# Two FFNs: sums of up-projection weight blocks made in HBM ahead of their tiles, and five more tiles by seven block products

## The chip, the core and the metric

One core of a Trainium2 chip runs the whole program. The metric is device time in microseconds (us) of one execution. All inputs lie in HBM when it starts; all arithmetic is in float32, which TensorE handles as float32r: each operand is split into a high and a low part, and a product takes three matmuls (high·high, high·low, low·high).

## The reference, cut to what matters

A two-layer decoder trunk on 512 tokens and 1024 features. Each layer has a mixer, then a gated FFN, then a gated per-layer embedding. The change is in the FFN, and in the weights that it loads:

```python
def conv_ffn(xn, w_up, conv_w, conv_b, w_down):        # xn: 512 x 1024
    h = xn @ w_up                                       # 1024 x 5632, gate half and linear half
    hp = jnp.pad(h, ((0, 0), (CONV_WIDTH - 1, 0), (0, 0)))
    c = conv_b + sum(hp[:, t:t + S] * conv_w[t] for t in range(CONV_WIDTH))
    g, u = jnp.split(c, 2, axis=-1)
    return (jax.nn.silu(g) * u) @ w_down                # 2816 x 1024
```

## The kernel before, in words

**Tiles.** The 2816 hidden features of an FFN are 22 tiles `j` of 128. For a tile, the kernel needs 256 columns of `w_up` (128 gate, 128 linear), which is 1 MB: 128 partitions by 8 blocks of input features by 2 blocks of 128 columns. The tiles go in three parts, 0-7, 8-15 and 16-21 (`PARTS`); after each part comes the product with the rows of `w_down` that belong to it. One tile of each next part (8 and 16) is computed ahead of that product.

**A plain tile** (`up`, `mm3`) takes 8 x 2 x 3 = 48 matmuls of 128x512, named `up` in the profile. **A woven tile** (`woven_up`) groups features and tokens in 2 x 2 blocks and takes seven block products instead of eight (Winograd's form of Strassen's scheme): 7 x 4 x 3 = 84 matmuls of 128x256, named `ux` and `uy`. For that it needs four combinations of the weight blocks, made by three adds of VectorE (`weave`, L163 to L165) into a buffer `wsum`. Its weights are split in four units, three of 1024 columns and one of 512, where a plain tile has two of 1024. Its results go to SBUF by five copies of ScalarE and two adds of VectorE (L812, L813; tiles `head` and `tail`, in the profile `gate`/`line` or `out..h`/`out..l`). Before, the tiles in `UPS` are woven in both layers: 7, 8, 9, 10, 12, 14, 16, 17, 18, 20, 21.

**Weights.** SyncE's queue brings pieces of 1 MB from HBM into three staging buffers (`staged`, `load`; `wraw`, and `wsum` takes one of the three too). Unit by unit, ScalarE casts the high part (`wh`, L203) and VectorE subtracts it for the low part (`wl`, L204) into a ring of four buffers each (`pump`, `WBUFS`), so that the split runs four units ahead of TensorE. A load starts once its staging buffer is free, that is when the last `wl` that reads it is done.

**Order.** Each engine runs its instructions in the order in which it is given them; `behind` pins an instruction behind another on one engine. GpSimd does little: norm sums (`nf0acc`, `np0acc`, `n1acc`), an inverse root for each norm (`nf0rt`, `n1rt`), and the DMAs on its own queue. Those on L600 add to what is at the destination (`accum_op=ALU.add`): `saved<-head`, `saved<-tail`, `h<-head`, `h<-tail`, of 256 KB each. The root `n1rt`, in the stage of the first layer's gate and the K projection, goes by VectorE's `n1hl` and `n1d` to a matmul `n1sp`, which spreads it over the partitions.

Of the kernel before, what the change touches and what calls it, by code (L numbers as in the profile page):

```python
# [52 lines left out]
def tile_yoco(ctx: ExitStack, tc: tile.TileContext, t, out: bass.AP, out_b: bass.AP):  # L53
    nc = tc.nc
# [13 lines left out]
        return mmp.tile([P, S], F32, tag="mm", name=name)  # L68


    pieces, paired, woven, beside = [], set(), set(), set()

    def plan(ap_, n, cols, own=None):
# [23 lines left out]
    def plan_woven(w, n_chunks, k0, k1):  # L97

        for c in range(n_chunks):
            n = (k1 - k0) * P  # L100
            woven.add(len(pieces))
            pieces.append((w[c, :, k0 * 256 : k1 * 256], 2 * n, [(0, n)] * 3 + [(0, n // 2)], None))

    def plan_ups(l, j0, j1):
        for j in range(j0, j1):
            (plan_woven if j in UPS else plan_cols)(t["w_up"][l, j : j + 1], 1, *((0, KD) if j in UPS else (KD,)))

    def plan_ffn(l):
        plan(t["pT"][l], 2 * S, S, own=[(mp, "m4", "m5")])
# [31 lines left out]
    state = {"raw": 0, "unit": 0, "next": 0, "tags": [0, 1, 2], "turn": 2, "pt": 0, "sent": {}}  # L141

    def behind(ins, front):

        tc.add_manual_dep(ins.ins, front.ins.name,
                          mybir.DependencyInfo(mybir.DependencyClass.NoSync, mybir.DependencyReason.DATA),
                          reason="order")

    def staged(name):
        tags = state["tags"]  # L150
        r = wp.tile([P, 2 * UNIT], F32, tag=f"r{tags[state['turn'] % len(tags)]}", bufs=1, name=name)
        state["turn"] += 1
        return r

    def weave(i, q):


        n = pieces[i][1] // 4
        g = raws[i][:, : 4 * n].rearrange("p (k b m) -> p b k m", b=4, m=P)
        if q == 0:  # L160
            s = sums[i] = staged(f"wsum{i}")[:, : 4 * n].rearrange("p (b k m) -> p b k m", b=4, m=P)
            k = n // P
            nc.vector.tensor_add(s[:, 0::3], g[:, 1:2].to_broadcast([P, 2, k, P]), g[:, 0::3])  # L163
            nc.vector.tensor_add(s[:, 2], s[:, 3], g[:, 0])
            nc.vector.tensor_add(s[:, 1], s[:, 2], g[:, 2])  # L165
        return (g[:, 0:3:2], sums[i][:, 2:4], sums[i][:, 0:2], g[:, 3:4])[q]

    def load(upto, queue=nc.sync):
        while state["raw"] < min(upto, len(pieces)):
            j = state["raw"]  # L170
            a, m = pieces[j][:2]
            r = raws[j - 1][:, UNIT:] if j in beside else staged(f"wraw{j}")
            ins = queue.dma_start(r[:, :m].rearrange("p (c m) -> p c m", c=2) if j in paired else r[:, :m], a)
            for front in state["sent"].pop(j, []):
                behind(ins, front)
            raws[j] = r
            state["raw"] += 1
# [145 lines left out]
    class Norm:  # L323
# [11 lines left out]
        def square(self, k, eng=None):  # L335
            sq = tp.tile([P, S], F32, tag="sq", name=f"{self.name}sq{k}")
            box["squared", k] = ins = nc.scalar.activation(sq, h[k], AF.Square)
            if self.acc is None:
                self.acc = sq
            else:  # L340
                acc = tp.tile([P, S], F32, tag="acc", name=f"{self.name}acc{k}")
                self.added = (eng or nc.gpsimd).tensor_add(acc, self.acc, sq)
                self.acc = acc
            return ins

# [99 lines left out]
        def rstd(self):  # L445

            r = tp.tile([P, S], F32, tag="rstd", name=f"{self.name}rstd")
            if self.line is not None:
                nc.gpsimd.dma_start(r, self.line.partition_broadcast(P))
            else:  # L450
                nc.scalar.copy(r, self.spread(0, S // 64))
            return r

    def inv_root(ms, name, scale=1.0, n=None):
        if n is None:
            n = ms.shape[1]
            ms = [(slice(None), ms)]
        m = const.tile([P, n], F32, tag=f"ms{n}", bufs=2, name=f"{name}m")
        for some, x in ms:
            box["m"] = nc.vector.tensor_scalar(m[some, :], x, scale, EPS, op0=ALU.mult, op1=ALU.add)  # L460
        r = const.tile([P, n], F32, tag=f"rt{n}", bufs=2, name=f"{name}rt")
        nc.gpsimd.tensor_tensor(r, m, minus_half[:, :n], op=ALU.pow)
        return r

    box = {}
# [264 lines left out]
    def ffn(l, norm, nxt):  # L730
# [56 lines left out]
        def woven_up(j, later):  # L787

            product = products(ins)
            n = PAIRS * P  # L790
            chain, other = psum(f"ux{j}")[:, first], psum(f"uy{j}")
            if j in ASIDE:
                head, tail = couple(ASIDE[j], f"out{j}", F32)
# [11 lines left out]
            nc.scalar.copy(side, other[:, second])  # L805
# [6 lines left out]
            nc.vector.tensor_sub(tail[:, second], tail[:, second], side)  # L812
            nc.vector.tensor_add(head, head, other)  # L813
            return (head, tail) if later else gated(j, (head, tail))
# [91 lines left out]
    def ple(l, norm, nxt, pe):  # L906
        xs = norm.xs[0][0]
        rstd, held = None, []
        for c in range(4):
            parts = chunk(256, KD)  # L910
# [114 lines left out]
    edge = at.tile([P, PAIRS, 2, N], F32R, tag="vtl", name="edge")  # L1025
    us = [Pair(c, edge, f"us{c}", range(3 * PAIRS)) for c in range(PAIRS)]
    for c in range(4):
        parts = chunk(256, KD)
        ups = [psum(f"u{c}_{j}") for j in range(2)]
        for j in range(2):  # L1030
# [47 lines left out]
    for k in range(KD):  # L1078
        nm.split(k, 1)
        if k == 3:  # L1080
            nm.turn()
    rt = nm.begin(rows=2)

    state["tags"] = [0, 1]
    parts = chunk(256, KD)
# [1 line left out]
    mm3(qps[0], parts, xq, 0)  # L1087
    rstd = nm.rstd()
    mm3(qps[1], parts, xq, P)

    for j in range(2):
        kf = tp.tile([P, S], F32, tag="acc", name=f"kf{j}")
# [314 lines left out]
    r = [f"r{(state['turn'] + j) % 3}" for j in range(3)]  # L1407
# [229 lines left out]
```

## Time and profile before

| | |
|---|---|
| median of 3 runs (lowest to highest) | 1100.43 us (1099.83 to 1101.02) |
| the profiled execution's own time | 1100.39 us |
| its span in the profile | 1098.7 us |
| granted TensorE clock | 0.999 |
| TensorE busy | 1089.1 us (99%) |
| VectorE busy | 959.0 us (87%) |
| ScalarE busy | 661.0 us (60%) |
| GpSimd busy | 125.0 us (11%) |
| moved by DMA | 144.24 MB, mean 131 GB/s |

A row of a group of instructions gives line, engine, operation, tiles and shapes, the count, then total busy us and mean ns of one. A row of a timeline gives start and length in us. In a row of waits stand the total, the times and the longest. A row by windows gives, after the stretch and its length, the busy time and count of PE, PEld, VectorE (DVE), ScalarE (ACT) and GpSimd (POOL), those that have instructions there, then granted clock, DMA share and GB/s. A row of DMA issues gives the count, KB of each and median us from issue to landing.

### The profile page before, as it was taken

The page shows a single profiled execution, that of the slowest core. Times are in us where ns is not written, and L with a number is a line of the kernel's source. Part 1 is how long each engine was busy: PE and PEld are TensorE (multiplying, and loading weights), DVE is VectorE, ACT ScalarE, POOL GpSimd, SP SyncE. Part 2 cuts the span into 40 slices and gives each one's busy share as a digit, 9 for nine tenths or more (in the row PEclk, how much of TensorE's full clock was granted, in tenths as well). Part 3 has the DMA queues.
Part 4 walks back from the last instruction along what each step waited for, and adds up shares of the span by engine and source line. Part 5 has one row for each costly group of instructions (what it writes and reads, how often), then busy time and mean ns, then how long its engine had stood idle before and what let it go on. Part 6 is the DMA issues. An engine that isn't in the chain of part 4 may idle for free.

```text
span 1098.7 us, 17476 instructions
## 1 busy us (share of the span) xinstructions
PE 1089.1 (99%) x6629; PEld 974.4 (89%) x6629; DVE 959.0 (87%) x1540; ACT 661.0 (60%) x1141; POOL 125.0 (11%) x192
## 2 busy tenths in 40 slices
PE   9999999999999999999999999999999999999997
PEld 7888988899998999988888887888999989999886
DVE  5588889999899989877988997799998999898887
ACT  5735666565676656655656775565655666567544
POOL 2200200000100010021114452000001000100200
PEclk9999999999999999999999999999999999999999
DMA  9621674125633267353234216441255333664534
GB/s 317 113 88 39 178 264 150 43 77 116 155 115 116 79 160 222 120 190 112 67 87 135 78 58 227 176 153 39 77 142 128 115 116 86 156 220 142 203 95 98
DMA packets 47508, 144.24 MB, mean 131 GB/s; under 512 B 13048, under 2 KB 18688, under 8 KB 36928
## 3 DMA queue, kind: packets, MB, share of 16 engines
q1 hardware_dynamic: 40560, 128.77, 35.6%
q0 software_dynamic: 5296, 9.70, 6.7%
q10 hardware_dynamic: 1568, 4.65, 1.1%
q8 instruction: 52, 0.85, 0.3%
q14 instruction: 32, 0.26, 0.1%
HBM read 116.89 MB, written 18.88 MB: 124 GB/s over the span
## 4 chain that ended last, share of the span: by engine, by line
PE 95%; DVE 2%; issue 1%; ACT 1%; DMA 0%; SPq 0%; POOLq 0%; POOL 0%; ACTq 0%
PE up L234 20%; PE ux L234 10%; PE dx L234 10%; PE uy L234 8%; PE dy L234 8%; PE d L234 6%; PE q L234 4%; PE gate L234 4%; PE u L234 4%; PE o L234 4%; PE up L750 2%; PE pv L1326 1%; PE v L244 1%; PE v L245 1%; PE v L246 1%; PE pin L234 1%
## 5 line engine op out<-in xcount | busy, mean ns | idle before, releaser
L204 DVE TENSOR_TENSOR wl<-wraw,wh 128x1024 fp32r<-128x1024 f32 (+2 forms) x198 | 217.3, 1102 | 42.8 <-ACT wh L203 41.9
L203 ACT CAST wh<-wraw 128x1024 fp32r<-128x1024 f32 (+2 forms) x197 | 182.8, 933 | 107.6 <-PE up L234 21.8
L203 ACT CAST wh<-wsum 128x1024 fp32r<-128x1024 f32 x84 | 88.3, 1052 | 62.7 <-issue 14.9
L204 DVE TENSOR_TENSOR wl<-wsum,wh 128x1024 fp32r<-128x1024 f32 x84 | 102.5, 1225 | 16.1 <-ACT wh L203 16.0
L762 DVE SCALAR_TENSOR_TENSOR c<-up,vec,c 128x511 f32<-128x511 f32 (+1 forms) x88 | 65.0, 744 | 2.4 <-ACT c L760 1.9
L234 PE MATMUL up<-nf10h,wh 128*128 128x512 f32 x160 | 62.3, 389 | 0.0
L234 PE MATMUL up<-nf00h,wh 128*128 128x512 f32 x160 | 62.3, 389 | 0.0
L234 PE MATMUL up<-nf10l,wh 128*128 128x512 f32 x160 | 62.3, 389 | 0.0
L234 PE MATMUL up<-nf00l,wh 128*128 128x512 f32 x160 | 62.3, 389 | 0.0
L234 PE MATMUL up<-nf00h,wl 128*128 128x512 f32 x160 | 62.1, 389 | 0.0
L234 PE MATMUL up<-nf10h,wl 128*128 128x512 f32 x160 | 62.0, 389 | 0.0
L600 POOL DMA_DIRECT2D saved<-head x16 | 13.9, 871 | 412.9 <-DVE head L720 412.9
L760 ACT ACTIVATE c<-up,vec 128x512 f32<-128x512 f32 x44 | 34.0, 777 | 31.8 <-PE up L234 26.6
L163 DVE TENSOR_TENSOR wsum<-wraw 128x1024 f32<-128x1024 f32 x42 | 51.2, 1220 | 0.6
L234 PE MATMUL ux<-t,wh 128*128 128x256 f32 x264 | 50.4, 283 | 0.0
L234 PEld LDWEIGHTS ux<-t,wh 128*128 128x128 f32 x264 | 41.2, 192 | 0.0
L234 PE MATMUL ux<-t,wl 128*128 128x256 f32 x132 | 37.4, 283 | 0.0
L234 PEld LDWEIGHTS up<-nf00h,wl 128*128 128x128 f32 x160 | 30.0, 188 | 6.2
L234 PEld LDWEIGHTS up<-nf10h,wl 128*128 128x128 f32 x160 | 30.0, 188 | 6.2
L234 PEld LDWEIGHTS up<-nf00l,wh 128*128 128x128 f32 x160 | 30.0, 188 | 6.2
L234 PEld LDWEIGHTS up<-nf10l,wh 128*128 128x128 f32 x160 | 30.0, 188 | 6.2
L234 PEld LDWEIGHTS up<-nf10h,wh 128*128 128x128 f32 x160 | 30.0, 188 | 6.0
(769 smaller groups left out, 3734.3 us busy)
## 6 DMA issues: line engine op xcount, KB each, us to landing
wraw<-in_w_up SPq DMA_DIRECT2D x44, 1024.0 KB, 5.6
wraw<-in_w_down SPq DMA_DIRECT2D x16, 1024.0 KB, 5.0
wraw<-in_w_gate SPq DMA_DIRECT2D x8, 1024.0 KB, 5.5
wraw<-in_w_down SPq DMA_DIRECT2D x8, 768.0 KB, 4.5
wraw<-in_w_u SPq DMA_DIRECT2D x4, 1024.0 KB, 9.4
wraw<-in_w_out SPq DMA_DIRECT2D x4, 1024.0 KB, 4.9
saved<-head POOLq DMA_DIRECT2D x16, 256.0 KB, 4.2
saved<-tail POOLq DMA_DIRECT2D x16, 256.0 KB, 4.1
```

Of the source, the lines that this page charges most:

```text
L163: nc.vector.tensor_add(s[:, 0::3], g[:, 1:2].to_broadcast([P, 2, k, P]), g[:, 0::3])
L203: cast = nc.scalar.copy(hi, src)
L204: state["split"] = splits[u] = cast, nc.vector.tensor_sub(low, src, hi.bitcast(F32))
L234: return [nc.tensor.matmul(ps, w, x, start=first and j == 0, stop=last and j == len(todo) - 1, skip_group_check=onto) for j, (w, x) in enu ...
L244: nc.tensor.matmul(ps, xh[:, s], wh[:, a:b], start=st, stop=False)
L245: nc.tensor.matmul(ps, xl[:, s], wh[:, a:b], start=False, stop=False)
L246: nc.tensor.matmul(ps, xh[:, s], wl[:, a:b], start=False, stop=en)
L600: box["onto"] = nc.gpsimd.dma_start(x, y, accum_op=ALU.add)
L750: nc.tensor.matmul(ps, w[:, off + s * P : off + (s + 1) * P], x, start=k == 0 and x is xh and w is wh, stop=k == KD - 1 and x is xl)
L760: nc.scalar.activation(c, ps, AF.Identity, bias=v("conv_b", l * 2 * NJ + col), scale=cw[2])
L762: ins = nc.vector.scalar_tensor_tensor(c[:, tap:], ps[:, : S - tap], cw[2 - tap], c[:, tap:], op0=ALU.mult, op1=ALU.add)
L1326: nc.tensor.matmul(ps, lhs, rhs, start=j == 0, stop=j == len(todo) - 1)
```

## The change

**Sums in HBM.** For eleven tiles (layer 0: 10 to 15; layer 1: 10 to 14) the four combinations of weight blocks are made in HBM, in four batches of three, three, two and three tiles. Each batch is a chain of steps: two plain copies on SyncE's queue (HBM to HBM, 256 KB for each tile), then on GpSimd's queue two accumulating DMAs, a plain copy, an accumulating one, a plain copy, an accumulating one, each of 256 KB for each tile, and each waiting for what it reads to have landed. For a batch of three tiles each DMA is 768 KB. Sources in `w_up` are read in runs of 512 B (1,536 of them in 768 KB). `BATCHES` says at which points of the program each step is emitted: for layer 0's tiles 10-12 during the mixer's `u` products; for 13-15 during layer 0's tiles 1-4; for layer 1's tiles 13-14 during layer 0's tiles 9-13; for layer 1's 10-12 during layer 0's gate, K and first Q products.

**Loads.** Such a tile is loaded by four DMAs instead of one into two staging buffers, 1.75 MB in all: two of the blocks and the sums. No add of VectorE is left for it. `flip` exchanges staging buffers before and after a run of such tiles.

**Seven products.** Tiles 11, 13 and 15 of layer 0 and 11 and 13 of layer 1, plain before, are woven now; of the others with sums in HBM, 10, 12 and 14 were woven before. `ASIDE` gives some tiles other homes for `head` and `tail`.

```diff
-UPS = (7, 8, 9, 10, 12, 14, 16, 17, 18, 20, 21)
-ASIDE = {7: 12, 9: 7, 17: 7, 20: 6}
+UPS = [(7, 8, 9, 10, 11, 12, 13, 14, 15, 16, 17, 18, 20, 21), (7, 8, 9, 10, 11, 12, 13, 14, 16, 17, 18, 20, 21)]
+ASIDE = [{7: 12, 9: 7, 11: 7, 13: 12, 15: 12, 17: 7, 20: 6}, {7: 12, 9: 7, 11: 7, 13: 12, 17: 7, 20: 6}]
+BATCHES = [
+    (0, 10, 13, [("u", 1), ("u", 1), ("u", 2), ("u", 2), ("u", 3), ("u", 3)]),
+    (0, 13, 16, [("up", 0, 1), ("up", 0, 2), ("up", 0, 3), ("up", 0, 3), ("up", 0, 4), ("up", 0, 4)]),
+    (1, 13, 15, [("up", 0, 9), ("up", 0, 10), ("up", 0, 11), ("up", 0, 11), ("up", 0, 13), ("up", 0, 13)]),
+    (1, 10, 13, [("gate", 0, 0), ("gate", 0, 1), ("gate", 0, 2), ("gate", 0, 3), ("k",), ("q",)]),
+]
...
+    def sums_ahead(l, j0, j1, keys):
+        n = KD // 2 * P
+        whole = dram.tile([(j1 - j0) * P, 4 * n], F32, name=f"sums{l}_{j0}")
+        w = t["w_up"][l, j0:j1].rearrange("j p (k b m) -> (j p) k b m", b=4, m=P)
+        s = {x: whole[:, i * n : (i + 1) * n].rearrange("r (k m) -> r k m", m=P) for i, x in enumerate((2, 3, 0, 1))}
...
+        def copy(x, y):
+            behind(nc.sync.dma_start(x, y), state["loaded"])
+
+        def onto(x, y):
+            behind(nc.gpsimd.dma_start(x, y, accum_op=ALU.add), box["onto"])
+
+        def then(x, y):
+            behind(nc.gpsimd.dma_start(s[x], s[y]), box["onto"])
+
+        steps = [lambda: [copy(s[x], w[:, :, 1]) for x in (3, 0)],
+                 lambda: [onto(s[x], w[:, :, x]) for x in (3, 0)],
+                 lambda: then(2, 3), lambda: onto(s[2], w[:, :, 0]),
+                 lambda: then(1, 2), lambda: onto(s[1], w[:, :, 2])]
+        for key, step in zip(keys, steps):
+            to_come.setdefault(key, []).append(step)
...
@@ weave
+        if i in summed:
+            a, c = raws[i]
+            return (a[:, : 2 * n].rearrange("p (k b m) -> p b k m", b=2, m=P),
+                    a[:, 2 * n :].rearrange("p (b k m) -> p b k m", b=2, m=P),
+                    c[:, : 2 * n].rearrange("p (b k m) -> p b k m", b=2, m=P),
+                    c[:, 2 * n : 3 * n].rearrange("p (b k m) -> p b k m", b=1, m=P))[q]
@@ load
+            if j in summed:
+                n = m // 4
+                if j - 1 not in summed:
+                    flip()
+                x, y = raws[j] = staged(f"wraw{j}"), staged(f"wsum{j}")
+                for there, here in ((x[:, : 2 * n].rearrange("p (k m) -> p k m", m=P),
+                                     a.rearrange("p (k m) -> p k m", m=P)[:, 0::2]),
+                                    (x[:, 2 * n :], summed[j][:, : 2 * n]),
+                                    (y[:, : 2 * n], summed[j][:, 2 * n :]),
+                                    (y[:, 2 * n : 3 * n].rearrange("p (k m) -> p k m", m=P),
+                                     a.rearrange("p (k m) -> p k m", m=P)[:, 3::4])):
+                    state["loaded"] = queue.dma_start(there, here)
...
@@ ffn
         def up(j, later=False):
-            if j in UPS:
+            come("up", l, j)
+            if j in UPS[l]:
                 return woven_up(j, later)
```

VectorE, layer 0, where tile 10's results are added up (`line`, `gate`) and the weights of the tiles behind it are split. Before, tile 11 is plain and tile 12 woven: the first row is the second and last unit of tile 11, and the three adds into `wsum` and the other two `wl` are tile 12's:

```order
L204 TENSOR_TENSOR wl_3271<-wraw_3238,wh_3270 128x1024
L312 TENSOR_TENSOR act_0_2l<-act_0u,act_0_2h 128x512
L163 TENSOR_TENSOR wsum_3303<-wraw_3299 128x2x512
L204 TENSOR_TENSOR wl_3302<-wraw_3299,wh_3301 128x1024
L164 TENSOR_TENSOR wsum_3303<-wsum_3303,wraw_3299 128x512
L812 TENSOR_TENSOR line_3207<-line_3207,side_3208 128x256
L165 TENSOR_TENSOR wsum_3303<-wsum_3303,wraw_3299 128x512
L813 TENSOR_TENSOR gate_3206<-gate_3206,uy_3205 128x512
L204 TENSOR_TENSOR wl_3340<-wsum_3303,wh_3339 128x1024
```

The same place in the changed kernel, where tile 11 is woven too; the first `wl` and the last two are its second, third and fourth unit:

```order
L276 TENSOR_TENSOR wl_3299<-wraw_3262,wh_3298 128x1024
L384 TENSOR_TENSOR act_0_2l<-act_0u,act_0_2h 128x512
L887 TENSOR_TENSOR line_3231<-line_3231,side_3232 128x256
L888 TENSOR_TENSOR gate_3230<-gate_3230,uy_3229 128x512
L276 TENSOR_TENSOR wl_3328<-wsum_3263,wh_3327 128x1024
L276 TENSOR_TENSOR wl_3369<-wsum_3263,wh_3368 128x512
```

The three adds that made sums are gone; behind `gate`, two more units of tile 11 are split, which it did not have as a plain tile.

GpSimd's queue in the stage of layer 0's gate and the K and first Q products, before. `n1acc` are the norm's sums, `n1rt` its root:

```order
L342 TENSOR_TENSOR n1acc_5472<-n1sq_5460,n1sq_5470 128x512
L342 TENSOR_TENSOR n1acc_5519<-n1acc_5472,n1sq_5517 128x512
L342 TENSOR_TENSOR n1acc_5556<-n1acc_5519,n1sq_5554 128x512
L342 TENSOR_TENSOR n1acc_5603<-n1acc_5556,n1sq_5601 128x512
L342 TENSOR_TENSOR n1acc_5640<-n1acc_5603,n1sq_5638 128x512
L462 TENSOR_TENSOR n1rt<-n1m,minus_half 128x8
```

The same stage in the changed kernel; L132 are accumulating DMAs, L135 plain copies, all of 768 KB:

```order
L414 TENSOR_TENSOR n1acc_5674<-n1sq_5662,n1sq_5672 128x512
L132 DMA sums_10_87<-in_w_up 384x4x128
L132 DMA sums_10_87<-in_w_up 384x4x128
L414 TENSOR_TENSOR n1acc_5723<-n1acc_5674,n1sq_5721 128x512
L414 TENSOR_TENSOR n1acc_5760<-n1acc_5723,n1sq_5758 128x512
L135 DMA sums_10_87<-sums_10_87 384x512
L414 TENSOR_TENSOR n1acc_5808<-n1acc_5760,n1sq_5806 128x512
L414 TENSOR_TENSOR n1acc_5845<-n1acc_5808,n1sq_5843 128x512
L132 DMA sums_10_87<-in_w_up 384x4x128
L536 TENSOR_TENSOR n1rt<-n1m,minus_half 128x8
L135 DMA sums_10_87<-sums_10_87 384x512
L132 DMA sums_10_87<-in_w_up 384x4x128
```

The first copy on GpSimd's queue stands between the third and fourth sum, and waits for the first accumulating DMA to have landed; the third accumulating DMA stands right ahead of `n1rt`, and waits for that copy. GpSimd's other work behind them waits as long.

More of the change, by code (lines that the diff above doesn't have):

```diff
@@ L102, in plan_woven, with come @@
             pieces.append((w[c, :, k0 * 256 : k1 * 256], 2 * n, [(0, n)] * 3 + [(0, n // 2)], None))
+    summed, far_sums, to_come = {}, {}, {}
+    def sums_ahead(l, j0, j1, keys):
[3 more added lines that the diff above has]
+        s = {x: whole[:, i * n : (i + 1) * n].rearrange("r (k m) -> r k m", m=P) for i, x in enumerate((2, 3, 0, 1))}
+        for j in range(j0, j1):
+            far_sums[l, j] = whole[(j - j0) * P : (j - j0 + 1) * P]
+        def copy(x, y):
[10 more added lines that the diff above has]
+            to_come.setdefault(key, []).append(step)
+    def come(*key):
+        for step in to_come.pop(key, []):
+            step()
+    for batch in BATCHES:
+        sums_ahead(*batch)
     def plan_ups(l, j0, j1):
         for j in range(j0, j1):
-            (plan_woven if j in UPS else plan_cols)(t["w_up"][l, j : j + 1], 1, *((0, KD) if j in UPS else (KD,)))
+            if (l, j) in far_sums:
+                summed[len(pieces)] = far_sums[l, j]
+            (plan_woven if j in UPS[l] else plan_cols)(t["w_up"][l, j : j + 1], 1,
+                                                       *((0, KD) if j in UPS[l] else (KD,)))
     def plan_ffn(l):
@@ L140, in tile_yoco, with flip @@
     raws, ready, splits, sums = {}, {}, {}, {}
[L141 to L147, printed above, removed]
+    state = {"raw": 0, "unit": 0, "next": 0, "tags": [0, 1, 2], "turn": -1, "pt": 0, "sent": {}}
+    def flip():
+        tags, i = state["tags"], state["turn"] + 1
+        a, c = i % 3, (i + 1) % 3
+        tags[a], tags[c] = tags[c], tags[a]
     def staged(name):
@@ L448, in rstd @@
             if self.line is not None:
-                nc.gpsimd.dma_start(r, self.line.partition_broadcast(P))
+                box["onto"] = nc.gpsimd.dma_start(r, self.line.partition_broadcast(P))
             else:
@@ L461, in inv_root @@
         r = const.tile([P, n], F32, tag=f"rt{n}", bufs=2, name=f"{name}rt")
-        nc.gpsimd.tensor_tensor(r, m, minus_half[:, :n], op=ALU.pow)
+        box["onto"] = nc.gpsimd.tensor_tensor(r, m, minus_half[:, :n], op=ALU.pow)
         return r
@@ L791, in woven_up @@
             chain, other = psum(f"ux{j}")[:, first], psum(f"uy{j}")
-            if j in ASIDE:
-                head, tail = couple(ASIDE[j], f"out{j}", F32)
+            if j in ASIDE[l]:
+                head, tail = couple(ASIDE[l][j], f"out{j}", F32)
             else:
@@ L909, in ple @@
         for c in range(4):
+            come("gate", l, c)
             parts = chunk(256, KD)
@@ L1027, in tile_yoco @@
     for c in range(4):
+        come("u", c)
         parts = chunk(256, KD)
@@ L1082, in tile_yoco @@
     rt = nm.begin(rows=2)
+    come("k")
     state["tags"] = [0, 1]
@@ L1089, in tile_yoco @@
     mm3(qps[1], parts, xq, P)
+    come("q")
     for j in range(2):
@@ L1406, in tile_yoco @@
     parts2 = chunk(S, KD, ahead=2 * WBUFS)
-    r = [f"r{(state['turn'] + j) % 3}" for j in range(3)]
+    r = [f"r{state['tags'][(state['turn'] + j) % 3]}" for j in range(3)]
     turned_b = squares(wp, r[0], "turned_b")
```

11 lines of the change are left out of this document (added).

## Prediction

> **What bounds the kernel now.** I read the page's busy times first, then PE's waits, then a table by windows of the stretch of tiles 9 to 16 (all five tiles that change form lie in it), once for each layer.
>
> ```profile
> PE 1089.1 (99%) x6629; PEld 974.4 (89%) x6629; DVE 959.0 (87%) x1540; ACT 661.0 (60%) x1141; POOL 125.0 (11%) x192
> PE idle L283 <- DVE minus_half L286: 1.1, 1, 1.1
> PE uy L234 <- ACT side L805: 0.3, 2, 0.2
> 290.70:375.10 84.40, 84.40 (x572) 77.97 (x572) 81.28 (x118) 55.64 (x90) 1.43 (x2) 1.00 0.34 108
> 838.50:922.90 84.40, 84.40 (x573) 77.97 (x572) 81.28 (x118) 55.59 (x90) 1.44 (x2) 1.00 0.34 108
> ```
>
> TensorE is the bound: 99% busy, its longest wait 1.1 us, and in both stretches busy for all 84.40 us at full granted clock. So only matmul time taken away from PE brings anything. But VectorE is busy 81.28 of the same 84.40 us (96%): it is the next bound, 3.1 us behind. ScalarE (55.6 of 84.4) and DMA (share 0.34) have room.
>
> **PE, part by part.** What does one conversion save?
>
> ```profile
> 165.47 64.37 PE up L234 x284
> 290.64 0.28 PE L234 MATMUL ux<-nf00h,wh 128*128 128x256 f32 x1
> 371.28 0.40 PE L234 MATMUL dx<-edge,wh 128*128 128x256 f32 x2
> 371.82 0.39 PE L234 MATMUL uy<-nf00h,wh 128*128 128x256 f32 x1
> 374.77 0.28 PE L234 MATMUL dx<-edge,wl 128*128 128x256 f32 x1
> 344.56 1.44 PE uy L234 x12
> ```
>
> The first row is a run of plain tiles: 64.37 us / 284 = 0.2267 us for a matmul of 512 columns, so a plain tile takes 48 x 0.2267 = 10.88 us. The stretch from tile 9's first matmul to the row at 374.77 is 84.13 us; 0.54 of it (371.28 to 371.82) belongs to the next product, so 83.59 us are five woven and three plain tiles: (83.59 - 3 x 10.88) / 5 = 10.19 us for a woven one, with what it waits for ScalarE's `side`. One conversion saves 10.88 - 10.19 = 0.69 us, five save 3.45. A woven tile that waits for nothing would take 84 x 1.44/12 = 10.08 us; then five save 4.0. I take 3.45, since `side` has its waits in the list above.
>
> **VectorE.** Where its adds go and what takes their place:
>
> ```profile
> L163 DVE TENSOR_TENSOR wsum<-wraw 128x1024 f32<-128x1024 f32 x42 | 51.2, 1220 | 0.6
> L164 DVE TENSOR_TENSOR wsum<-wsum,wraw 128x512 f32<-128x512 f32 x42 | 28.8, 686 | 0.5
> L165 DVE TENSOR_TENSOR wsum<-wsum,wraw 128x512 f32<-128x512 f32 x42 | 28.8, 686 | 0.5
> L204 DVE TENSOR_TENSOR wl<-wsum,wh 128x1024 fp32r<-128x1024 f32 x84 | 102.5, 1225 | 16.1 <-ACT wh L203 16.0
> L204 DVE TENSOR_TENSOR wl<-wraw,wh 128x512 fp32r<-128x512 f32 x46 | 32.2, 701 | 17.5 <-ACT wh L203 17.5
> 313.89 0.41 DVE L812 TENSOR_TENSOR line<-line,side 128x256 f32<-128x256 f32 x1
> 314.83 0.68 DVE L813 TENSOR_TENSOR gate<-gate,uy 128x512 f32<-128x512 f32 x1
> ```
>
> Sums in HBM take 1.220 + 0.686 + 0.686 = 2.59 us off each of tiles 10, 12 and 14: 7.78 us in each layer. A converted tile needs one unit of 1024 and one of 512 more, 1.225 + 0.701 = 1.93, and the two adds of its results, 0.41 + 0.68: 3.02 us. So layer 0 (three conversions) adds 9.05 and nets +1.3: 82.5 us of work, in a stretch that PE would do in 84.40 - 3 x 0.69 = 82.3. Layer 1 (two) adds 6.03 and nets -1.7: 79.5 us in 83.0. There VectorE has more room than before; in layer 0 it has none, and PE can be held. What it loses is at least nothing (VectorE enters the stretch ahead of PE), at most the whole 2.07 of layer 0.
>
> ```profile
> 341.94 1.22 DVE L204 TENSOR_TENSOR wl<-wsum,wh 128x1024 fp32r<-128x1024 f32 x1
> ```
>
> How far is it ahead? This is tile 14's third unit, split by 343.16; PE's row at 344.56, shown above, starts that tile's twelve-matmul groups of 1.44 us, and uses the unit after three of them, at 348.88. The lead is 5.7 us, more than the 0.2 us that layer 0 lacks, and more than a few waits for ScalarE's casts (the largest idle of the `wl` groups above, some 16 us in the whole program). I take 0.5 us, for single late units.
>
> ScalarE gets, for each conversion, a cast of 1024 (1.05 us in a row below), one of 512, and five copies for two: some 10 us in layer 0, an estimate, on 55.6 of 82. That costs nothing, as long as its 27 us of idle time cover it.
>
> **Weight loads.** A tile with sums brings 1.75 MB instead of 1, through the same three buffers.
>
> ```profile
> 291.56 0.68 DVE L204 TENSOR_TENSOR wl<-wraw,wh 128x512 fp32r<-128x512 f32 x1
> 299.54 1.05 ACT L203 CAST wh<-wsum 128x1024 fp32r<-128x1024 f32 x1 [1.13 <-PE uy L234]
> wraw<-in_w_up SPq DMA_DIRECT2D x44, 1024.0 KB, 5.6
> wraw<-in_w_u SPq DMA_DIRECT2D x1, 1024.0 KB, 13.3
> n0line<-n0rt POOLq DMA_DIRECT2D x1, 2.0 KB, 11.0
> ```
>
> The tightest is tile 10's second buffer: free when tile 9's last unit is split (292.24), wanted by the cast at 299.54. That gives 7.3 us for 768 KB, where 1 MB takes 5.6. It costs nothing as long as that holds. By bytes the stretch's share rises from 0.34 to about 0.60, with the third batch's traffic on top. The next buffers come free about one tile (10 us) ahead of use.
>
> **GpSimd's queue.** The trace has no accumulating DMA of 768 KB; the nearest rows:
>
> ```profile
> saved<-tail POOLq DMA_DIRECT2D x16, 256.0 KB, 4.1
> hT<-turned_a SPq DMA_DIRECT2D x16, 64.0 KB, 2.0
> ```
>
> Call its time a. From below, an ordinary load's pace: 0.75 x 5.6 = 4.2 us. From the accumulating row, 2.0 us fixed (what 64 KB take) and 2.1 for 256 KB: 2.0 + 3 x 2.1 = 8.3 us. From above, if the number of pieces counts (1,536 of 512 B against 128 of 2 KB in `saved`): 2.0 + 12 x 2.1 = 27.2 us. I take 8.3, from the only row that accumulates. The Trainium skill (DMA: Bandwidth & Descriptors, "Anatomy of one DMA — SWDGE (gpsimd) path") gives 2.0 us plus bytes by 436 GB/s, which would be an estimated 3.8 us for 768 KB; for 256 KB it gives 2.6, and the trace's accumulating row of 4.1 does not agree, so I do not go by it.
>
> Who waits behind these DMAs? `n1rt`, in the gate stage:
>
> ```profile
> 518.21 1.30 POOL L342 TENSOR_TENSOR n1acc<-n1sq,n1sq 128x512 f32<-128x512 f32 x1 [11.20 <-ACT n1sq L337]
> 555.27 2.68 POOL L462 TENSOR_TENSOR n1rt<-n1m,minus_half 128x8 f32<-128x8 f32 x1 [16.08 <-DVE n1m L460]
> 558.58 0.68 DVE L417 TENSOR_TENSOR n1d<-pick,n1hl 128x512 fp32r<-128x512 f32 x1
> 559.46 0.40 PE L421 MATMUL n1sp<-n1d,ones 128*128 128x512 f32 x1
> ```
>
> Two accumulating DMAs go out behind the first sum (519.5); the copy behind them waits until what it reads has landed, and the third accumulating DMA, right ahead of `n1rt`, waits for the copy. With some 5 us for the copy (a load of 1 MB took 5.6) and 1 for issuing, 2a + 6 must fit into 555.27 - 519.5 = 35.8: a up to 14.9 us costs nothing. Each us beyond costs 2, and goes on to PE, as `n1d` ends 0.2 us ahead of `n1sp`. With 8.3 there are 13 us to spare.
>
> ```profile
> 53.90 1.05 POOL L462 TENSOR_TENSOR vrt<-vm,minus_half 128x4 f32<-128x4 f32 x1 [0.58 <-DVE vm L460]
> 112.13 0.96 POOL L600 DMA_DIRECT2D h<-head  x1 [57.18 <-ACT head L694]
> 258.72 0.92 POOL L600 DMA_DIRECT2D saved<-head  x1 [109.58 <-DVE head L720]
> 382.71 0.86 POOL L600 DMA_DIRECT2D saved<-head  x1 [89.86 <-DVE head L720]
> ```
>
> The other batches stand in idle times of GpSimd of 57, 110 and 90 us: the first needs 3a + 10 = 35 of 57, the others less than half. SyncE's eight plain copies wait for nothing, and stand ahead of loads that are needed later by more than the few us they take. All that: nothing.
>
> **The sum.** 1100.39 (the profiled execution; the median, 1100.43, is the same) - 3.45 + 0.5 = 1097.4 us.
>
> **The rivals.** *GpSimd's queue holds PE* (slower). If accumulating from pieces of 512 B goes by pieces and not by bytes, `n1rt` comes 2 x (a - 14.9) late. It decides from a = 14.9 on, and the gain is eaten at a = 16.4; a = 20 gives 1097.4 + 10.2 = 1107.6, the upper bound 27.2 gives 1122. For it: twelve times the pieces, and the `n0line` row, where 2 KB on GpSimd's queue took 11.0 us beside loads. Against it: 16 rows `saved` at 4.1, in the midst of loads.
>
> *Late weights* (slower). The `in_w_u` load above took 13.3 us beside other traffic, not 5.6. If tile 10's second load does, beside the third batch, it lands 6 us past its 7.3, about the lead of 5.7; with the same at the batch's next steps, PE waits some 6 us in layer 0: 1097.4 + 6 = 1103.4. It decides once loads take twice their usual time. For it: these two rows. Against it: a share of 0.60 leaves room, and later buffers have 10 us. The Trainium skill has the rule behind it (DMA: Bandwidth & Descriptors, "Issuing engines are not separate DMA queues"): all queues run on the same 16 DMA engines and interleave there. The 13.3 us row agrees; it speaks against this change, whose tiles with sums bring 1.75 times the bytes and whose batches come on top.
>
> *VectorE sets the pace in layer 0* (no change). It has 82.5 us of work for 82.3. If its waits for casts remain and the lead is gone at the start, the stretch stays at 84.4 and layer 1's 2 x 0.69 alone is left: 1100.39 - 1.38 = 1099.0.
>
> **How the numbers follow.** The forecast has 0.58, VectorE's pace 0.14, GpSimd's queue 0.17, late weights 0.11. A measurement of this kernel can tell about 0.2% (2.2 us) from no change: faster is below 1098.2, slower above 1102.6. So faster 0.58, same 0.14, slower 0.28. The range begins at the full saving without loss, 1100.39 - 4.0 = 1096.4, less the 0.6 by which single runs of the kernel before differ from their median: 1095.8. Above, it takes in VectorE's pace and late weights, and of GpSimd's queue the part up to a = 19.5 (1097.4 + 9.2 = 1106.6), some half of that case: 0.09 is left out there, and some 0.05 below. The forecast's own range is 1095.8 to 1098.2.
>
> **What would show it.** Right: `up` has 5 x 48 = 240 matmuls fewer, `ux` and `uy` 420 more; the two stretches take about 82.3 and 83.0 us with PE's waits as few as now; VectorE's busy time in them is about 82.5 and 79.5; no add into `wsum` for the tiles with sums; accumulating DMAs land in about 8 us; `n1rt` starts when `n1m` is done. Wrong: accumulating DMAs of 15 us and more with `n1rt` released by one of them; loads of sums at 10 us and more with PE waiting for `wl` behind `wh` behind a DMA; a stretch of layer 0 at 84 with VectorE at 100%.

## The result, and the profile after

The changed kernel takes 1103.76 us (median of 9 runs, 1101.71 to 1105.08), the kernel before 1100.43 (9 runs, 1099.47 to 1101.02): ratio 1.0028, 95% interval 1.0019 to 1.0037. It is 3.3 us slower, where 3.0 us faster was forecast. The profiled execution took 1101.84 us (span 1100.1), one of the shortest of the nine, so its trace shows only a part of the loss.

The page's busy times and TensorE's waits of the changed kernel:

```profile
PE 1088.1 (99%) x6809; PEld 982.2 (89%) x6809; DVE 960.6 (87%) x1542; ACT 674.9 (61%) x1176; POOL 159.2 (14%) x216
PE uy L306 <- ACT side L880: 1.0, 1, 1.0
PE dx L306 <- DVE wl L276: 1.0, 1, 1.0
```

TensorE is busy 1.0 us less (1089.1 before), not 3.4, and has two waits of 1.0 us that it did not have. Where are they? GpSimd's `saved<-head` that follows the last add of a product with `w_down` is a good mark on either side of the stretch of tiles 9 to 16. Of the kernel before:

```profile
290.39 0.86 POOL L600 DMA_DIRECT2D saved<-head  x1 [1.65 <-DVE head L720]
414.38 0.86 POOL L600 DMA_DIRECT2D saved<-head  x1 [1.64 <-DVE head L720]
838.21 0.86 POOL L600 DMA_DIRECT2D saved<-head  x1 [1.64 <-DVE head L720]
962.22 0.86 POOL L600 DMA_DIRECT2D saved<-head  x1 [1.65 <-DVE head L720]
```

And of the changed kernel:

```profile
290.58 0.85 POOL L674 DMA_DIRECT2D saved<-head  x1 [1.66 <-DVE head L794]
415.74 0.86 POOL L674 DMA_DIRECT2D saved<-head  x1 [1.65 <-DVE head L794]
839.54 0.86 POOL L674 DMA_DIRECT2D saved<-head  x1 [1.47 <-DVE head L794]
962.54 0.86 POOL L674 DMA_DIRECT2D saved<-head  x1 [1.65 <-DVE head L794]
```

From mark to mark layer 0 takes 125.16 us instead of 123.99, layer 1 123.00 instead of 124.01: layer 1 gains 1.0, layer 0 loses 1.2. The rest of this execution's 1.4 us is outside, at the start (0.2) and behind layer 1's last mark (1.1).

Layer 0 by windows of 10 us, with the columns of the tables above; first the kernel before, then the changed one:

```profile
291.00:301.00 10.00, 10.00 (x85) 9.90 (x84) 8.70 (x13) 6.49 (x12) 1.12 (x2) 1.00 0.68 162
361.00:371.00 10.00, 10.00 (x73) 9.45 (x72) 9.27 (x16) 6.69 (x11) 0.00 (x0) 1.00 0.30 105
371.00:381.00 10.00, 10.00 (x85) 9.90 (x84) 9.91 (x14) 7.48 (x14) 0.00 (x0) 1.00 0.31 107
```

```profile
291.00:301.00 10.00, 10.00 (x84) 9.90 (x84) 6.54 (x10) 6.47 (x12) 4.42 (x4) 1.00 0.99 194
361.00:371.00 10.00, 10.00 (x84) 9.79 (x83) 10.00 (x14) 6.72 (x12) 0.00 (x0) 1.00 0.31 105
371.00:381.00 10.00, 8.01 (x65) 7.60 (x64) 10.00 (x16) 7.33 (x13) 0.00 (x0) 1.00 0.17 48
```

VectorE is busy 2.16 us less at the head of the stretch, and at its end it is busy for all of 20 us while TensorE stands for 2. So it has run out of its lead. In the chain that ended last, VectorE stands without TensorE from 353.2 us until TensorE's second wait ends at 376.0; two of its pieces, and TensorE's matmuls behind them:

```profile
353.49 1.74 DVE wl L276 x2
374.82 1.15 DVE wl L276
376.01 1.44 PE dx L306 x10
```

Why did it not work ahead at the head? Its timeline, and ScalarE's:

```profile
297.78 1.23 DVE L276 TENSOR_TENSOR wl<-wraw,wh 128x1024 fp32r<-128x1024 f32 x1 [1.35 <-ACT wh L275]
296.71 1.05 ACT L275 CAST wh<-wraw 128x1024 fp32r<-128x1024 f32 x1 [0.99 <-PE uy L306]
```

VectorE waits 1.35 us for a cast, and the cast waits for TensorE to free a buffer of the ring: the split is four units ahead and can go no further. Before, VectorE made tile 10's sums in that time, for which the ring needs no place. The time that the change takes from it there is time for which it has no other use. (This is read from the windows; no run gives tile 10's adds alone back to VectorE.)

GpSimd's queue did not hold `n1rt`, and its DMAs took a little longer than forecast (the median of twelve):

```profile
sums<-in_w_up POOLq DMA_DIRECT2D x12, 768.0 KB, 9.9
556.61 2.70 POOL L536 TENSOR_TENSOR n1rt<-n1m,minus_half 128x8 f32<-128x8 f32 x1 [14.15 <-DVE n1m L534]
```

### The profile page after: what moved, and what is told of

Its sections match the earlier page's. It is cut to its first block, busy times and chain, and to the rows that moved or that the text cites. A ratio compares the mean times of both kernels' runs of the same rounds, so it can differ in the third digit from the quotient of the medians.

```text
span 1100.1 us, 18007 instructions
## 1 busy us (share of the span) xinstructions
PE 1088.1 (99%) x6809; PEld 982.2 (89%) x6809; DVE 960.6 (87%) x1542; ACT 674.9 (61%) x1176; POOL 159.2 (14%) x216
## 4 chain that ended last, share of the span: by engine, by line
PE 88%; DVE 6%; DMA 2%; issue 2%; ACT 1%; SPq 1%; POOL 0%; POOLq 0%; DVEq 0%; ACTq 0%
PE up L306 15%; PE ux L306 12%; PE dx L306 10%; PE uy L306 10%; PE dy L306 8%; PE q L306 4%; PE gate L306 4%; PE u L306 4%; PE o L306 4%; PE d L306 3%; PE up L825 2%; PE pv L1405 1%; DVE wl L276 1%; PE v L316 1%; PE v L318 1%
## 5 line engine op out<-in xcount | busy, mean ns | idle before, releaser
L275 ACT CAST wh<-wraw 128x1024 fp32r<-128x1024 f32 (+2 forms) x197 | 185.2, 945 | 99.9 <-PE up L306 15.5
L837 DVE SCALAR_TENSOR_TENSOR c<-up,vec,c 128x511 f32<-128x511 f32 (+1 forms) x68 | 50.1, 744 | 2.2 <-ACT c L835 2.0
L306 PE MATMUL up<-nf10h,wh 128*128 128x512 f32 x128 | 49.9, 390 | 0.0
L306 PE MATMUL up<-nf00h,wh 128*128 128x512 f32 x112 | 43.7, 390 | 0.0
L306 PE MATMUL up<-nf00l,wh 128*128 128x512 f32 x112 | 43.6, 390 | 0.0
L306 PE MATMUL up<-nf00h,wl 128*128 128x512 f32 x112 | 43.5, 390 | 0.0
L132 POOL DMA_DIRECT2D sums<-in_w_up x16 | 30.6, 2054 | 52.4 <-DMA sums<-sums 47.0
L843 ACT ACTIVATE a<-c 128x512 f32<-128x512 f32 x44 | 27.8, 631 | 16.8 <-DVE c L837 16.8
L306 PE MATMUL uy<-nf00h,wh 128*128 128x256 f32 x112 | 33.0, 294 | 1.2 <-ACT side L880 1.0
L1349 ACT ACTIVATE prs<-prs,neg 128x129 f32<-128x129 f32 x64 | 25.3, 397 | 13.3 <-DVE neg L1344 12.4
L844 DVE TENSOR_TENSOR a<-a,c 128x512 f32<-128x512 f32 x44 | 30.3, 688 | 3.5 <-ACT a L843 2.0
```

The lines of the kernel that those rows point to most:

```text
L132: behind(nc.gpsimd.dma_start(x, y, accum_op=ALU.add), box["onto"])
L275: cast = nc.scalar.copy(hi, src)
L306: return [nc.tensor.matmul(ps, w, x, start=first and j == 0, stop=last and j == len(todo) - 1, skip_group_check=onto) for j, (w, x) in enu ...
L837: ins = nc.vector.scalar_tensor_tensor(c[:, tap:], ps[:, : S - tap], cw[2 - tap], c[:, tap:], op0=ALU.mult, op1=ALU.add)
L843: box["silu"] = nc.scalar.activation(a, cs[0], AF.Silu)
L844: nc.vector.tensor_mul(a, a, cs[1])
```

## The experiments

Two theories stood against each other. **Pace**: VectorE sets the end of layer 0's stretch, since its third conversion has no room. **Traffic**: transfers of the batches and the loads of 1.75 MB make weights late. In the table, "by" is the difference of the medians to the kernel before on the same chip, with the ratio's interval, and the two stretches are from mark to mark in the profiled execution (before 123.99 and 124.01).

| run | median us | by | ratio, 95% | layer 0 | layer 1 |
|---|---|---|---|---|---|
| `again` | 1103.57 | +3.1 | 1.0021 to 1.0046 | 124.97 | 123.03 |
| `layer1_only` | 1099.15 | -1.3 | 0.9977 to 0.9995 | 124.00 | 123.03 |
| `layer0_only` | 1102.95 | +2.5 | 1.0013 to 1.0030 | 124.96 | 124.00 |
| `sums_unused` | 1101.16 | +0.7 | 0.9997 to 1.0015 | 124.00 | 124.00 |
| `two_in_0` | 1099.83 | -0.4 | 0.9986 to 1.0003 | 123.02 | 124.01 |
| `later_batch` | 1102.98 | +2.8 | 1.0015 to 1.0035 | 124.97 | 124.01 |
| `adds_stay` | 1112.05 | +11.8 | 1.0095 to 1.0126 | 134.22 | 124.01 |
| `sums16` | 1104.76 | +4.1 | 1.0023 to 1.0050 | 122.61 | 124.27 |
| `sums16_later` | 1100.83 | +0.5 | 0.9993 to 1.0011 | 122.63 | 124.27 |
| `move3` | 1102.72 | +2.1 | 1.0011 to 1.0029 | 124.97 | 123.00 |
| `best` | 1102.30 | +1.7 | 1.0007 to 1.0025 | 123.00 | 123.06 |
| `best_move3` | 1100.36 | -0.3 | 0.9995 to 1.0013 | 123.03 | 123.03 |
| `best_later` | 1101.33 | +1.0 | 1.0000 to 1.0018 | 123.02 | 122.99 |
| `after_later` | 1102.30 | +1.5 | 1.0007 to 1.0025 | 124.95 | 123.02 |

### Each layer alone

`layer1_only` has `UPS[0]` and `ASIDE[0]` as before and the last two of `BATCHES`; `layer0_only` has `UPS[1]` and `ASIDE[1]` as before and the first two.

> Layer 0 as before the change, layer 1 with its two batches and two conversions. Pace theory: layer 1's stretch keeps its gain of 1.0 us, nothing else is lost: about 1099.4. Traffic theory: the third batch, beside layer 0's tiles 9 to 13, or the fourth makes loads late: 1100.4 to 1102, with a stall of TensorE behind a load.

> Layer 0 with its two batches and three conversions, layer 1 as before the change. Pace theory: layer 0's stretch loses what it lost in the changed kernel, 1.2 us: about 1101.6, with TensorE's stall at tiles 15 and 16. Traffic theory: without the third batch beside the stretch the loads come in time, TensorE does not stall there and gains: 1098.5 to 1099.5.

Layer 1 alone gains 1.3 us, 1.0 of it in its stretch; it is faster than both kernels. Layer 0 alone loses 2.5, 0.97 of it in its stretch, with the same two waits of TensorE, and with no third batch beside it. In the stretch the pace theory holds for both; the further 1.5 us of layer 0 it does not give.

### What VectorE's microseconds are worth in layer 0

`two_in_0`, on top of `layer0_only`, leaves tile 15 plain:

```diff
-    (0, 13, 16, [("up", 0, 1), ...
+    (0, 13, 15, [("up", 0, 1), ...
```

> Layer 0 alone is changed, and as layer 1 is in the changed kernel: sums for tiles 10 to 14, tiles 11 and 13 converted, tile 15 plain; layer 1 as before. Pace theory (VectorE ran out of lead at the third conversion): the stretch is 1.0 us shorter than before instead of 1.0 longer, so 2.0 below the run with layer 0 alone (1102.95): 1100.9; what is left above 1099.4 then comes from the batches. Traffic theory (late loads of sums make the stretch long): the stretch stays longer than before, 1102 to 1103.

`adds_stay` is `layer0_only` with `BATCHES = []`: tiles 11, 13 and 15 are converted, and VectorE makes all sums.

> Layer 0 with its three conversions, but no sums in HBM: VectorE makes all combinations, weights come as 1 MB loads; layer 1 as before. Pace theory: VectorE has 3 x (3.02 + 2.59) = 16.8 us more than before in the stretch, of which 3.1 idle and the lead of 5.7 take up at most 8.8, and the 2.07 less of TensorE's work come on top: 8 us or more later, 1108 to 1114. Traffic theory: without batches and long loads, the three conversions gain up to 2: 1098.5 to 1100.

`sums16` is `layer0_only` with `(0, 13, 17, ...)`: tile 16's sums come from HBM too.

> Layer 0 alone with its three conversions, and tile 16's combinations made in HBM too (second batch of four tiles), so that VectorE loses 2.59 us of adds right ahead of the place where TensorE stalled. Pace theory: the stall of 2 us goes, and the three conversions bring their 0.49 each: the stretch is 1.0 to 1.5 us shorter than before instead of 1.0 longer, the time 1102.95 - 2.2 = 1100.7 or less. Traffic theory: one more tile of 1.75 MB and a longer batch: 1103 or more, the stretch no shorter.

The stretch answers each time as the pace theory says. One conversion fewer: 123.02 instead of 124.96. Three tiles' adds put back and three more tiles' adds on top, 15.5 us of VectorE more than in `layer0_only` (the batches' transfers go with it): 134.22, and TensorE waits for `wl` and, behind it, `side`:

```profile
PE uy L302 <- ACT side L876: 4.1, 3, 3.1
PE ux L302 <- DVE wl L272: 3.3, 2, 2.8
```

And 2.59 us of VectorE less, right ahead of the stall (`sums16`): 122.61, by a window around the stall of the changed kernel; first the changed kernel, then `sums16`, which is some 5 us later there. Its list of TensorE's waits has neither of the two of 1.0 us:

```profile
350.00:385.00 35.00, 33.01 (x269) 32.17 (x268) 34.68 (x50) 24.34 (x42) 0.86 (x1) 1.00 0.27 91
350.00:385.00 35.00, 34.90 (x289) 34.39 (x288) 34.64 (x51) 27.01 (x46) 0.00 (x0) 1.00 0.44 141
```

All three conversions pay in the stretch then, 1.4 us. (Layer 1's stretch, not changed in this kernel, is 0.3 longer in both runs with tile 16's sums; why was not looked into.) Yet the whole of `sums16` is 4.1 us slower than before: its expectation of 1100.7 failed, for a reason outside the stretch.

### The first weights of an FFN

TensorE's longest wait in `sums16`, and the row of ScalarE that it follows from:

```profile
PE up L823 <- ACT nf00h L512: 3.3, 1, 3.3
164.65 1.04 ACT L273 CAST wh<-wraw 128x1024 fp32r<-128x1024 f32 x1 [4.70 <-DMA wraw<-in_w_up]
```

The cast of layer 0's weights stands on ScalarE ahead of the normed features `nf00h`, and waits 4.70 us for a load. In SyncE's queue the second batch's two plain copies (key `("up", 0, 1)`) come right ahead of that load. The queue of the kernel before, then of the changed one:

```profile
146.83 0.33 SPq L173 DMA_DIRECT2D wraw<-in_w_up  x1
```

```profile
144.67 2.29 SPq L129 DMA_DIRECT2D sums<-in_w_up  x2
147.06 3.53 SPq L244 DMA_DIRECT2D wraw<-in_w_up  x1
```

The load is issued in its time, but takes 3.53 us to issue instead of 0.33, behind copies that are still under way: the first accumulating DMA, which waits for one of them, starts at 151.80. A second profile of the changed kernel, `again` (the same kernel), has the stall too, in the chain that ended last:

```profile
147.14 14.92 DMA wraw<-in_w_up
162.14 1.05 ACT wh L275
163.18 0.53 ACT nf00h L514
163.75 3.01 PE up L825 x12
```

> The changed kernel once more, for a second profile of it. Pace theory (VectorE sets the pace in layer 0's stretch of tiles 9 to 16): TensorE stalls some 3 us at tiles 15 and 16 there, as in the first profile, and nowhere else; the time is then near 1102. Traffic theory (transfers of the sums are late in some runs): this profile shows a stall of 1 to 3 us at another place, behind a load, and the time is 1103 to 1105.

The load lands 14.9 us after its issue, where the row of loads before has 5.6, and TensorE waits 0.9 us. Of the seven profiles with these copies of 768 KB (of the changed kernel, `layer0_only`, `sums_unused` and `move3`), only this one has the wait; in the first profile the load landed just in time. Two more runs move the second batch behind these weights, to `[("up", 0, 3), ("up", 0, 3), ("up", 0, 4), ("up", 0, 4), ("up", 0, 5), ("up", 0, 5)]`: `later_batch` from `layer0_only`, `sums16_later` from `sums16`.

> Layer 0 alone, with its three conversions; the second batch begins at tile 3 instead of tile 1 and ends at tile 5 instead of 4, so that its two plain copies no longer stand in SyncE's queue ahead of the FFN's first weights. Traffic theory: those weights land in time in every run, 0.5 to 1 us less than 1102.95: 1102.0 to 1102.4, and the single runs closer together. Pace theory alone: no change, 1102.9.

> Layer 0 with three conversions and tile 16's sums as in the run before (1104.76), and the second batch begun at tile 3 instead of tile 1, behind the FFN's first weights. Theory of the copies ahead (the batch's plain copies stand in SyncE's queue ahead of a load that TensorE needs at once): TensorE's wait of 3.3 us for the first up tile goes, the stretch stays 1.4 us shorter than before: 1100.4 - 1.4 + 0.6 = 1099.6. Rival (the longer batch costs wherever it stands): 1102 or more.

In `sums16_later` the wait is gone, and with it 3.9 us of time: 1100.83, still 1.2 above its expectation. From `nf0rt` to the first mark it takes 142.89 us, against 147.85 in `sums16` and 142.91 before. That the second batch with DMAs of 1 MB, begun ahead of the first weights, holds TensorE is shown. How much of it its copies do and how much the two accumulating DMAs behind them, which also run beside the load, the runs do not separate. With 768 KB the way from `nf0rt` to the first mark is longer in one profile of seven, by 1.2 us, and `later_batch` (1102.98 against 1102.95) shows that it is not what `layer0_only` usually loses.

### The batches without use, and the third batch

`sums_unused` makes all four batches, and has tiles and loads of the kernel before (`if False:` ahead of `summed[len(pieces)] = ...`).

> All four batches are made in HBM, but no tile reads them: tiles, loads and VectorE's adds as in the kernel before. Pace theory: the batches cost nothing by themselves: 1100.4, within 0.5. Traffic theory: the batches' own transfers delay loads or norms: 1101.5 to 1103, with the single runs further apart than before's 1.5 us.

Its 0.7 us is within what the measurement can tell from nothing (0.9997 to 1.0015). `best` has tiles 10 to 14 with sums and 15 plain in both layers; `move3` is the changed kernel, and `best_move3` is `best`, with the third batch at other keys:

```diff
-    (1, 13, 15, [("up", 0, 9), ("up", 0, 10), ("up", 0, 11), ("up", 0, 11), ("up", 0, 13), ("up", 0, 13)]),
+    (1, 13, 15, [("up", 1, 1), ("up", 1, 2), ("up", 1, 3), ("up", 1, 3), ("up", 1, 4), ("up", 1, 4)]),
```

> The changed kernel with the third batch (layer 1's tiles 13 and 14) moved from layer 0's tiles 9 to 13 to layer 1's tiles 1 to 4. Pace theory: the stretch of layer 0 is as long as before, 1103.6 stays. Traffic theory (the third batch's transfers beside loads of 1.75 MB make some loads late, in some runs): near the sum of the two layers' effects, 1100.4 + 2.5 - 1.3 = 1101.6, and the runs closer together.

> The changed kernel without layer 0's third conversion: tiles 10 to 14 have sums in both layers, 11 and 13 are converted, 15 is plain in both. Pace theory: both stretches 1.0 us shorter than before, and the batches' 0.6 as in the runs with one layer: 1100.3 - 0.4 - 1.3 = 1098.6. Traffic theory: the third batch meets the long loads as in the changed kernel: 1100 or more.

> As the run before it, and the third batch moved to layer 1's tiles 1 to 4. Pace theory: the same, 1098.6. Traffic theory: this one only reaches 1098.6, at least 0.8 below the one with the third batch beside layer 0's long loads.

Moving the third batch takes 1.0 us off the difference of the changed kernel (+3.1 to +2.1) and 1.9 off that of `best` (+1.7 to -0.3). The intervals overlap a little in both pairs, but both point one way: beside the loads of 1.75 MB in layer 0 this batch seems to cost 1 to 2 us, as the traffic theory says. But what waits there is in no trace: in every profile of `best` and of the changed kernel the stretch is as long as without it. `best` alone, by the pace theory 1098.6, missed by 3.7.

`best_later` (from `best`) and `after_later` (from the changed kernel) have the second batch at tiles 3 to 5 of layer 0 and the third at tiles 3 to 5 of layer 1.

> Two conversions in each layer, second and third batch both begun at tile 3 of a layer's first part (the second in layer 0, the third in layer 1), away from the first weights of an FFN and from loads of 1.75 MB. Theory of the copies ahead: 1100.4 - 2.0 + 0.5 = 98.9 above 1000, that is 1098.9 or less, with single runs closer together. Rival (a cost of the batches that their place does not change): 1100.4 as in the run with the third batch moved.

> All five conversions of the changed kernel; the second batch begun at tile 3 of layer 0, the third at tile 3 of layer 1. Theory of the copies ahead: the two stretches (+1.0 and -1.0) and the 0.6 after the last output that the profiles of kernels with both layers changed have in common are left: 1101.0 to 1101.5, 2 us below the changed kernel. Rival (a cost that the places of these batches do not change): 1102.7 to 1103.6, as the changed kernel or the run with the third batch moved alone.

`after_later` gives back half of the loss (+3.3 to +1.5), a little less than expected; `best_later` misses by 2.4 us, and is no better than `best_move3`. The places of the two batches are a part of what lies outside the stretches, not all.

### More profiles

`best_look`, `again_look` and `before_look` are one more profile each of `best`, of the changed kernel and of the kernel before, `layer0_look` of `layer0_only`.

> One more profile of the kernel with two conversions in each layer and all batches in their place, whose runs went from 1100.05 to 1104.34. Theory of the copies ahead: where it is over 1102, TensorE waits 0.5 us or more behind a load of weights that a batch's transfers stand ahead of or run beside. Rival: the loss lies in the stretch of tiles 9 to 16, which would be longer than 123.0 us from the last add of one product to that of the next.

> One more profile of the changed kernel. The same two theories: waits behind loads outside the stretch, at the FFN's first weights, at the last w_down load and the K weights, where a batch's transfers are; or a stretch longer than 125.2 us.

> The kernel with layer 0 alone once more, for a second profile: its first was its fastest run of eleven. Pace theory: the stretch is 1.0 us longer than before as in the first. Traffic theory: 1 us or more is lost at another place, behind a load of weights that a batch's transfers stand ahead of or run beside.

> The kernel before once more, for a second profile. If the last product of layer 1 varies by itself, it takes more than 96.1 us from the last add of layer 1's first product to the last norm's root here too, up to 97 and more; if it is the change that disturbs it, 96.1 again.

The stretches are the same as in the first profiles (`best_look` 123.01 and 123.03, `again_look` 124.99 and 122.99, `layer0_look` 124.95, `before_look` 124.03 and 124.00). Between the profiles of the changed kernel (1101.84, 1104.61, 1101.43) other parts move. From layer 1's last mark to `np1rt`, the root of the norm behind its FFN, the kernel before takes 96.12 and 96.25 us, the changed one 96.46, 96.84 and 97.06, `later_batch` 97.66, `best_move3` 98.16, where no batch runs; `adds_stay`, which has no batch at all, takes 96.81.

In some profiles a load is behind such a loss. The last loads of `w_down` in a layer take at most 6.6 us from issue to landing in both profiles of the kernel before. In `later_batch` one takes 7.4 us there in layer 1, and a cast of ScalarE waits 1.9 us for it. In layer 0, `again` and `sums16_later` have the same, with 7.4 and 7.8 us, and the root of the norm behind that FFN comes 0.6 and 1.0 us later. No batch moves at these times, so that transfers beside these loads are not the reason; what is, was not found. `again` loses 0.6 us more up to `n1rt`, behind a load of the K weights, which took 5.1 us before and runs here beside an accumulating DMA of the fourth batch. Two loads and `n1rt` in the chain of `again`:

```profile
460.65 7.36 DMA wraw<-in_w_down
548.70 6.95 DMA wraw<-in_w_kv
558.72 2.71 POOL n1rt L536
```

What follows the last output's issue is longer too, in the changed kernel:

```profile
1095.47 0.34 ACTq L1632 DMA_DIRECT2D out<-yt  x1
```

From there to the end of the span it is 4.6 us; before, by the row below and its span of 1098.7, 3.9.

```profile
1094.78 0.35 ACTq L1553 DMA_DIRECT2D out<-yt  x1
```

And where layer 0 has two conversions, the attention of layer 1 has a new wait, in `two_in_0` and the four profiles of `best`, `best_move3` and `best_later`; TensorE's row in `two_in_0`, and a piece of the chain that ended last ahead of it:

```profile
PE o L304 <- ACT oh L1417: 0.9, 1, 0.9
668.11 0.83 DVE own_m L274
```

This piece is VectorE's split of a load of `pT`, which a later stage uses. It stands on VectorE ahead of the `side` that `oh` is cast from; in the kernel before it comes at 677.3 us, behind this place, and SyncE's queue brings `pT` behind the last output weights instead of ahead of them. That the staging buffers go round in another order with tile 15 plain is a possible reason, but was not tried.

## Why the prediction was wrong

Between the forecast of 1097.4 and the measured 1103.76 lie 6.4 us: 3.0 in the two stretches (2.6 in layer 0, 0.4 in layer 1), and 3.3 outside them, where the prediction had put nothing ("All that: nothing"). The runs show the cause of the first part, and of the second only pieces.

**The step that failed: VectorE's price in layer 0.** The work was counted rightly as too much (net +1.3 us), and then weighed as a sum over the whole stretch against a lead of 5.7 us, for 0.5. But time taken from VectorE is of use only where it can do something else. Tile 10's adds were made while the ring was full; without them it idles (8.70 to 6.54 us busy in 10), and the conversions' work comes later, where nothing is idle. The stretch became 1.0 us longer (124.95 to 125.16 in the eight profiles with three conversions and sums for tiles 10 to 15), where 2.07 - 0.5 = 1.6 were to be gained: 2.6 us. The rival "VectorE sets the pace" named the engine and the place, but took the old length of the stretch as its worst. The sign that the prediction had named for it came: in the last 20 us VectorE is busy 100%, and the stretch is not shorter.

**TensorE's gain per conversion was mis-sized.** Forecast 0.69 us, measured 0.5 (two conversions: 0.97 in `two_in_0`, 1.0 in layer 1). From one woven tile's group to that of the next but one, before and after:

```profile
302.45 1.44 PE uy L234 x12
323.59 1.44 PE uy L234 x12
```

```profile
302.64 1.44 PE uy L306 x12
323.38 1.44 PE uy L306 x12
```

A woven and a plain tile took 21.14 us, two woven ones take 20.74: 0.40 for this pair. The average of 10.19 us came from woven tiles with plain neighbours; between two woven ones it is 20.74 / 2 = 10.37. What it takes beyond the 10.08 us of its matmuls was not looked into. Five conversions at 0.49 would bring 2.4 us, not 3.45, even without a stall. For layer 1 the forecast of 1.4 us was close: 1.0 in the stretch, 1.3 in all when it is changed alone.

**GpSimd's queue: right where it was weighed.** The accumulating DMA of 768 KB took 9.9 us (median), forecast 8.3. In the stage of `n1rt` none of those ahead of it took more than 13.4, and the bound was 14.9; `n1rt` waits for `n1m` and not for a DMA of the batch (in `again` `n1m` itself is 0.6 us late, behind a load of weights). Among the weight loads of layer 0's first tiles one took 21.8 us, where TensorE does not wait for it. The estimate that rested on the Trainium skill (DMA: Bandwidth & Descriptors, "Anatomy of one DMA — SWDGE (gpsimd) path"), 3.8 us, was far off: the measurement decides.

**SyncE's copies: wrong at nothing.** "Needed later by more than the few us they take" did not hold for the load behind the second batch's copies: it took 14.9 us in one profile of seven, and TensorE waited 0.9 us. Rival "late weights" had the mechanism (loads at twice their time) and the size of a load (13.3 us), but at another place: in the stretch itself the loads came in time in every profile, though the DMA share there was 0.80 (from 291 to 376 us; 0.99 in the first window) and not 0.60. That its 1103.4 us are near the measured 1103.76 is luck. The Trainium skill's rule that all queues share the same DMA engines (DMA: Bandwidth & Descriptors, "Issuing engines are not separate DMA queues") agrees with the trace: from 143 to 165 us SyncE's weight loads took 11.3 us beside the batch, 6.1 before, and GpSimd's accumulating DMAs 19.6.

**What stays open.** The two stretches together cost the changed kernel nothing (+1.0 and -1.0). Its 3.3 us lie outside. The mean of its three profiled executions is 2.2 us above the kernel before: 0.7 behind the last output, 0.6 in the last product of layer 1, 0.4 by the first weights, 0.2 each in the last product of layer 0 and in the stage of `n1rt`. The usual execution loses 1.1 us more, and where it does the traces do not settle. By `after_later` about half of the whole goes with the places of the second and third batch. `adds_stay`, which has no batch, is 11.8 us slower with a stretch 10.2 longer, so that not all of it need be the batches' traffic; but its granted clock (0.994 to 0.997, against 0.997 to 0.999 of the kernel before) is lower too.

## What to carry to other kernels

Work taken from an engine that runs ahead through a ring helps only where the ring lets it use the time: look in each window what the engine does instead, and not at the sum over the stretch. A saving per tile measured beside other neighbours is to be measured again between the neighbours that it will have. And transfers that wait for nothing themselves are not free where they stand ahead of the first load of a stage, or run beside it.

## What the runs showed of the hardware that was not expected

An accumulating DMA of 768 KB from pieces of 512 B took 9.9 us (median of 12; the longest, beside weight loads, 21.8), of 512 KB beside long loads 13.4 (median of 4); issuing one of them kept GpSimd for about 1.9 us, where the 256 KB of `saved` take 0.86. With no transfer of the change near it, the time behind the last output's issue still grew from 3.9 us (both profiles of the kernel before) to 4.6 (all three of the changed one).
